# A hybrid decoder block on one core: the first stage pinned to a listed order on each engine, u products in halves, and the last tiles scaled on two engines

## The chip, the cores and the metric

The kernel runs on one core of one Trainium2 chip. The metric is the device time of one execution in microseconds (us). It is given as the median of several runs. The engines have short names: PE (TensorE, matrix products and transpositions), PEld (its weight loads), DVE (VectorE), ACT (ScalarE), POOL (GpSimd) and SP (SyncE, which issues most of the DMAs).

## The reference

The block takes `x` of 1024 tokens by 1024 channels and `mem` of 256 tokens by 1024 channels, all float32. Cut to its main lines:

```
u = rms_norm(x, norm_mix)
u_ssm, q, k, v, f_logit, gates = split(u @ w_in)          # widths 512, 512, 512, 512, 8, 2048
y = gelu(s5_ssm(u_ssm, ...))                              # diagonal state-space scan over the tokens
a, b = split(y @ w_glu);  out_a = a * sigmoid(b)
out_b = forgetting_attention(q, k, v, f_logit + b_forget) @ w_fox_o
ga, gb = split(sigmoid(gates))
h = x + (ga * out_a + gb * out_b) @ w_mix_out
h = h + cross_attention(rms_norm(h), rms_norm(mem, norm_mem_kv), w_mem_q, w_mem_kv, w_mem_o)
fa, fb = split(rms_norm(h) @ w_ffn_in)
h = h + (silu(fa) * fb) @ w_ffn_out
out = rms_norm(h) * norm_final
```

The part that matters first is how the stage at the head of the kernel makes `u` (transposed), the product `u_ssm`, and the keys and values of the memory tokens from `w_mem_kv`. The part that matters last is the final `rms_norm`.

## The kernel before, in words

**Splitting.** Products keep nearly float32 precision by splitting each operand into a high part (a cast to the reduced type float32r) and a low part (the difference). `split` (L176) makes both: ACT casts the high part (L177), and DVE, or POOL where that is asked for, subtracts it from the source (L178). A product of one 128-deep slice is then three matmuls (`mm3`, L165 to L169): high by high, high by low, low by high.

**Order.** The kernel is written in a framework that draws the instructions up at compile time. It gives every engine one queue of instructions in a fixed order, and adds the waits. Its scheduler goes by the order of the program as a priority, but lets a later instruction go ahead where an earlier one is, by its own estimate of durations, not ready yet. A helper can keep instructions behind a given one on the same engine (`behind`, L145).

**The first stage** (`stage_in`, L334 to L466) is a list of short steps, `ORDER_IN` (L41 to L47), carried out in that order by a table of functions (L456 to L466). A letter names the step and the rest its operands; `m` and `n` are the two memory tiles of 128 tokens and 0 to 7 the tiles of `x`:

- `F` fetches a tile; `G` fetches a gain row, and `B` spreads it over the 128 partitions with two small products on PE (L365) and two copies on ACT (L367).
- `Q` squares a tile on ACT and sums along the row (L373). `R` makes the reciprocal root (`rsqrt`, L186 to L203): an addition on DVE, the power on POOL (L196), and one Newton step of three small DVE instructions. One root serves one memory tile, or two tiles of `x`. `S` scales the tile by root and gain, on DVE (L216), or with `g` on ACT and POOL (L213, L214).
- `T` transposes half a tile (4 blocks of 128 by 128) into a PSUM bank on PE (L222); `E` evacuates that bank by splits into `uT` (or `mT`), a quarter tile of 128 by 256 each for `x`. The first half of a tile of `x` goes through the only bank called `misc`, the second through the two called `pv`.
- `D` fetches a block of weights: 0 to 3 are columns of `w_mem_kv` for the four heads' keys, 4 to 7 rows of it for the values, 8 to b the four blocks of 128 columns of `w_in` that make `u_ssm`. `W` splits it (with `g`, the low part on POOL). There are two buffers called `raw`, one called `xraw`, and four pairs for the split weights, so `W` waits until the product that used the pair four blocks earlier is done. The u weights (8 to b) were split through a permuted view, columns regrouped from (g n) to (n g).
- `K`, `V` and `U` are products. `K` is one head's keys (24 matmuls of 256 columns), `V` a quarter of the values (12 matmuls of 512 columns), `U` one block q of 128 channels of `u_ssm` for one half h of the tokens (24 matmuls of 512 columns). `k`, `v` and `u` bring the results out of PSUM.
- `Z` stores two of the four key and value tiles to DRAM. They share four slots (tag `kv`) with the gain rows before them and with the `us` tiles behind them, so the first `u` copies wait for the stores of `Z`.
- `u` (L446 to L452) copies a product to `us` on ACT, and after its second half stores block q to the DRAM tile `u_d` with one DMA of 512 KB.
- `X12` issues 12 small products whose result is not used, ahead of the first transpositions. `L0` fetches the parameters of the state-space branch (14 DMAs), `L1` transposes them on PE, and `P` carries out one piece of the preparation of that branch (`prepare`, from L1289, mostly small DVE instructions).

**The next stage** (`stage_ssm`, from L469) goes through 32 gate products of 24 matmuls each. Between them stand the steps of the state-space branch for each of the four blocks q: its weights on POOL and DVE (`weights`), the transposition of those (`turn_weights`, L1456, the first of them before the fifth gate product), the states (`states`, which reads `u_d` into `xg`, L1480), and the output.

**The last loop** (from L1160) is the second product of the feed-forward block, by seven sub-products (`ORDER` in L1102) over 11 pairs p, accumulated in eight PSUM banks. `o_add` (L1131 to L1136) adds a bank into the residual tile `Hf`, `square` (L1138) sums its squares on ACT, and `finish` (L1142 to L1149) makes the root, scales both halves of the tile on DVE by root and final gain (L1147), and stores each half with a DMA on SP (L1149). The last sub-product (n = 3) is finished tile by tile: for each of the tiles 0 to 3 its last nine matmuls, the sum, the squares, and `finish`.

Of the kernel before, what the change touches and what calls it, by code (L numbers as in the profile page):

```python
# [9 lines left out]
F32 = mybir.dt.float32  # L10
# [9 lines left out]
P = 128  # L20
# [46 lines left out]
def f32(ap):  # L67
    return ap.bitcast(F32)
# [47 lines left out]
        return self.pool.tile([P, 512], dt, tag="half", bufs=5, name=name)  # L116


class Block:
    BANKS = {"mm": 3, "sc": 2, "pv": 2, "misc": 1}  # L120

# [53 lines left out]

    def split(self, hi, lo, src, pool_lo=False):  # L176
        self.copied = self.A.copy(hi, src)  # L177
        (self.G if pool_lo else self.V).tensor_sub(lo, src, f32(hi))  # L178

    def rstd(self, src):  # L180
        ss = self.small.tile([P, 2], F32, name="ss")
# [36 lines left out]
    def turn(self, xs, b, bank):  # L218

        ps = self.bank(bank)  # L220
        for k in range(4):
            self.T.transpose(ps[:, k * P:(k + 1) * P], xs[:, (4 * b + k) * P:(4 * b + k + 1) * P], self.ident)  # L222
        return ps

    def turned(self, ps, b, act, t):
# [9 lines left out]
    def warm(self, n):  # L235

        ps = self.bank("misc")
        one = self.ident.bitcast(BF16)
        for _ in range(n):
            self.T.matmul(ps[:, :2 * P], one[:, :P], one, start=True, stop=True)  # L240


    def exp_parts(self, tile_, X):
# [90 lines left out]
def stage_in(B, xp, s5, x, mem, g_mix, g_kv, w_in, w_mem_kv, uT, u_d, kv_d):  # L334
# [8 lines left out]
    row, tiles, gain, ss, rs, raw, w, ps, us, kv = {}, {}, {}, {}, {}, {}, {}, {}, [], []  # L343
    names = {"m": -2, "n": -1, **{str(t): t for t in range(NT)}}

    def xtile(name="xt"):
# [13 lines left out]
    def gain_rows(i):  # L360
        gain[i] = xtile("gain")
        for c in range(2):
            cs = slice(512 * c, 512 * c + 512)
            p_ = B.bank("sc")
            T.matmul(p_, ones, row[i][:, cs], start=True, stop=True)  # L365
            with B.behind(B.copied if i else None):
                A.copy(gain[i][:, cs], p_)  # L367

    def square(t):
        if t % 2 == 0:  # L370
            ss[t // 2] = small.tile([P, 2], F32, name="ss2")
        with B.behind(B.copied if t in (0, 1) else None):
            A.activation(junk, tiles[t], AF.Square, scale=1.0 / 32, accum_out=ss[t // 2][:, t % 2:t % 2 + 1])  # L373

    def root(i):
        rs[i] = B.rsqrt(ss[-1][:, i % 2:i % 2 + 1] if i < 0 else ss[i])
# [48 lines left out]
    def kv_store(i0):  # L425
        for i in range(i0, i0 + 2):
            S.dma_start(kv_d[i], f32(kv[i]))
# [11 lines left out]
            cs = slice(t * 512, (t + 1) * 512)  # L439
            B.split(kv[2][:, cs], kv[3][:, cs], ps.pop(("v", t)))  # L440

    def ssm_in(q, h):
        ps["u", q, h] = B.bank("mm")
        B.gemm_t(ps["u", q, h], *w[8 + q], uT, h, 8)

    def ssm_out(q, h):  # L446
        if h == 0:
            us.append(xp.tile([P, D], F32, tag="kv", bufs=4, name="us"))
        uv = us[q].rearrange("p (t c) -> p t c", t=8)
        A.copy(uv[:, :, 64 * h:64 * h + 64], ps.pop(("u", q, h)).rearrange("p (c t) -> p t c", t=8))  # L450
        if h == 1:
            S.dma_start(u_d[q].rearrange("t p c -> p t c"), uv)  # L452

    prep = s5.prepare()

# [6 lines left out]
            "v": lambda a: values_out(), "Z": lambda a: kv_store(int(a)), "U": lambda a: ssm_in(int(a[0]), int(a[1])),  # L462
            "u": lambda a: ssm_out(int(a[0]), int(a[1])), "L": lambda a: s5.load(int(a)),
            "P": lambda a: next(prep, None), "X": lambda a: B.warm(int(a))}
# [75 lines left out]
def stage_tail(B, big, s2, sh, x, glu, aT, gate_d, kv_d, sums_d, w_fox_o, w_mix_out, g_mq, w_mem_q, w_mem_o, g_ffn,  # L540
# [563 lines left out]
    ops, Hf = {}, {}  # L1104
    ssq = small.tile([P, 2 * NT], F32, name="ssq", bufs=1)

    def o_get(m, behind=None):
# [23 lines left out]
    def o_add(n, i):  # L1131

        t, c, op = {1: (0, 0, ALU.add), 2: (0, 0, ALU.add), 6: (4, 0, ALU.add), 7: (4, 1, ALU.subtract),
                    5: (4, 1, ALU.subtract), 4: (4, 0, ALU.add), 3: (0, 1, ALU.subtract)}[n]
        h = Hf[t + i][:, 512 * c:512 * c + 512]
        V.tensor_tensor(out=h, in0=h, in1=sets[n in (2, 7, 4)][i], op=op)  # L1136

    def square(t, c):  # L1138
        A.activation(B.junk, Hf[t][:, 512 * c:512 * c + 512], AF.Square, scale=1.0 / 32,
                     accum_out=ssq[:, 2 * t + c:2 * t + c + 1])  # L1140

    def finish(t):  # L1142

        r = B.rsqrt(ssq[:, 2 * t:2 * t + 2], parts=2)
        for c in range(2):
            cs = slice(512 * c, 512 * c + 512)
            V.scalar_tensor_tensor(out=Hf[t][:, cs], in0=Hf[t][:, cs], scalar=r, in1=gfin[:, cs], op0=ALU.mult,  # L1147
                                   op1=ALU.mult)
            S.dma_start(out[t * P:(t + 1) * P, cs], Hf[t][:, cs])  # L1149
# [10 lines left out]
    for m, (n, p) in enumerate(seq):  # L1160
        if n == 3 and p >= NP - LAST:
            break
        for i in range(4):
            o_mm(m, i)
        if m + AHEAD < len(seq):
            o_get(m + AHEAD)
        if n < 3 and p in (2, 4, 6, 8):
            t = 4 * (n - 1) + p // 2 - 1
            Hf[t] = slot(name="hf")
            S.dma_start(Hf[t], h_d[t])  # L1170
        if p == NP - 1:
            for i in range(4):
                o_add(n, i)
                if n in (2, 5):
                    square(i if n == 2 else 4 + i, n // 3)
                if n == 4:
                    square(4 + i, 0)
                    finish(4 + i)
    for i in range(4):
        for m in range(len(seq) - LAST, len(seq)):  # L1180
            o_mm(m, i)
        o_add(3, i)
        square(i, 1)
        finish(i)


class Glu:
# [753 lines left out]
```

## Time and profile before

| | |
|---|---|
| time, median of 3 runs | 1569.69 us (1565.22 to 1571.21) |
| the profiled execution | 1565.22 us, span 1563.5 us |
| PE busy | 1524.3 us, 97% of the span |
| DVE, ACT, POOL busy | 1056.3, 679.0, 242.9 us |
| mean granted clock of PE | 0.992 |
| PE busy in the first 100 us | 87.3 us |
| first gate product on PE | at 104.14 us |
| last matmul ends | at 1553.24 us |

The profile is one execution. A view by groups gives, for each line and shape, the count, the busy time, the mean duration of one instruction, and the idle time of its engine just before, with what ended most of it. The view of waits says which line of an engine stood waiting and for which line of another. The timeline lists instructions by their start, with their length. The view by stretches gives each engine's busy time in a window, and PE's granted clock, the share of time in which the DMA engines were busy, and what they moved.

### The profile page before, as it was taken

How to read it: one execution, taken by the hardware profiler on the slowest of the kernel's cores; microseconds unless marked ns; L12 is line 12 of the kernel's file. 1: busy time of each engine (PE TensorE's matmuls, PEld its weight loads, DVE VectorE, ACT ScalarE, POOL GpSimd, SP SyncE). 2: the span in 40 equal slices, each digit the busy share in tenths (PEclk: the TensorE clock that was granted, in tenths of full speed). 3: DMA queues.
4: the chain of work that ended last, by engine and by line, in shares of the span. 5: the costliest groups of instructions: out<-in, count | busy, mean ns of one | idle time of the engine just before them, and what ended most of it. 6: DMA issues, size and time to landing. Idle time of an engine off the chain costs nothing.

```text
span 1563.5 us, 20462 instructions
## 1 busy us (share of the span) xinstructions
PE 1524.3 (97%) x7261; PEld 1250.4 (80%) x7261; DVE 1056.3 (68%) x1893; ACT 679.0 (43%) x1203; POOL 242.9 (16%) x323
## 2 busy tenths in 40 slices
PE   8899999999999899999999999999999999999997
PEld 6688888898777668888788778888888888888886
DVE  5947655544788786789756787777777766565555
ACT  6523333422566553444445654333333333354342
POOL 3135343200212122220102100000000000100001
PEclk9999999999999999999999999999999999999999
DMA  8655557642123637778431366444444554896642
GB/s 253 145 134 103 172 157 164 186 140 31 21 50 48 177 94 223 258 230 323 146 107 55 135 244 221 155 155 161 162 162 157 160 162 154 293 381 221 195 148 108
DMA packets 202586, 257.66 MB, mean 165 GB/s; under 512 B 35994, under 2 KB 127034, under 8 KB 201972
## 3 DMA queue, kind: packets, MB, share of 16 engines
q1 hardware_dynamic: 195860, 240.62, 51.4%
q10 hardware_dynamic: 6624, 15.73, 2.7%
q8 instruction: 57, 0.93, 0.2%
q14 instruction: 45, 0.37, 0.1%
HBM read 175.04 MB, written 83.20 MB: 165 GB/s over the span
## 4 chain that ended last, share of the span: by engine, by line
PE 82%; DVE 7%; DMA 4%; ACT 3%; issue 2%; POOL 2%; SPq 0%; DVEq 0%; POOLq 0%; ACTq 0%
PE mm L981 15%; PE pv L981 8%; PE mm L167 7%; PE mm L168 7%; PE mm L169 7%; PE mm L1128 5%; PE sc L1128 4%; PE sc L981 3%; PE pv L1128 3%; PE sc L169 2%; PE sc L168 2%; PE sc L167 2%; PE misc L1128 2%; PE mm L627 1%; PE pv L167 1%
## 5 line engine op out<-in xcount | busy, mean ns | idle before, releaser
L178 DVE TENSOR_TENSOR wlo<-raw,whi 128x1024 fp32r<-128x1024 f32 (+2 forms) x126 | 133.8, 1065 | 101.7 <-ACT whi L177 101.4
L177 ACT CAST whi<-raw 128x1024 fp32r<-128x1024 f32 (+2 forms) x127 | 115.9, 915 | 134.7 <-PE mm L168 36.0
L167 PE MATMUL mm<-uh,whi 128*128 128x512 f32 x344 | 137.5, 400 | 0.8 <-ACT whi L177 0.7
L178 DVE TENSOR_TENSOR ol<-or,oh 128x1024 fp32r<-128x1024 f32 x73 | 89.2, 1224 | 69.8 <-ACT oh L177 68.4
L169 PE MATMUL mm<-uh,wlo 128*128 128x512 f32 x344 | 135.4, 394 | 0.5 <-DVE wlo L178 0.5
L168 PE MATMUL mm<-ul,whi 128*128 128x512 f32 x344 | 135.5, 394 | 0.0
L177 ACT CAST oh<-or 128x1024 fp32r<-128x1024 f32 x73 | 76.8, 1053 | 100.3 <-PE mm L1128 33.3
L1013 POOL TENSOR_TENSOR g<-a,c 128x512 f32<-128x512 f32 x22 | 36.2, 1644 | 381.7 <-ACT a L1012 335.3
L196 POOL TENSOR_TENSOR r<-ms,mhalf 128x1 f32<-128x1 f32 (+1 forms) x30 | 21.7, 726 | 382.1 <-DVE ms L192 351.6
L1756 POOL TENSOR_TENSOR pl<-pf,ph 128x512 fp32r<-128x512 f32 (+1 forms) x32 | 39.5, 1236 | 243.4 <-DVE ph L1755 197.3
L169 PEld LDWEIGHTS mm<-uh,wlo 128*128 128x128 f32 x344 | 65.1, 189 | 14.8 <-DVE wlo L178 1.5
L167 PEld LDWEIGHTS mm<-uh,whi 128*128 128x128 f32 x344 | 65.3, 190 | 13.2 <-ACT whi L177 1.2
L168 PEld LDWEIGHTS mm<-ul,whi 128*128 128x128 f32 x344 | 65.1, 189 | 11.0
L1753 ACT ACTIVATE pf<-sc 128x512 f32<-128x512 f32 (+1 forms) x96 | 46.6, 490 | 46.9 <-DVE sc L1749 28.0
L981 PE MATMUL pv<-S3h,we 128*128 128x512 f32 x176 | 58.2, 390 | 0.1
L1759 DVE TENSOR_TENSOR pl<-pf,ph 128x512 fp32r<-128x512 f32 (+2 forms) x64 | 35.1, 549 | 10.0 <-ACT ph L1758 9.3
L1128 PE MATMUL mm<-oh 128*128 128x512 f32 x106 | 41.2, 389 | 0.0
L1128 PE MATMUL mm<-ol,oh 128*128 128x512 f32 x106 | 41.2, 389 | 0.0
L1128 PE MATMUL mm<-oh,ol 128*128 128x512 f32 x106 | 41.2, 389 | 0.0
L167 PE MATMUL mm<-yh,whi 128*128 128x512 f32 x104 | 41.1, 395 | 0.0
L168 PE MATMUL mm<-yl,whi 128*128 128x512 f32 x104 | 40.9, 393 | 0.0
L169 PE MATMUL mm<-yh,wlo 128*128 128x512 f32 x104 | 40.8, 393 | 0.0
(701 smaller groups left out, 4560.7 us busy)
## 6 DMA issues: line engine op xcount, KB each, us to landing
or<-c_d SPq DMA_DIRECT2D x77, 256.0 KB
wo<-in_w_ffn_out_dram SPq DMA_DIRECT2D x22, 512.0 KB
c_d<-g SPq DMA_DIRECT2D x44, 256.0 KB
t_d<-wo SPq DMA_DIRECT2D x44, 256.0 KB
or<-t_d SPq DMA_DIRECT2D x44, 256.0 KB
raw<-in_w_ffn_in_dram SPq DMA_DIRECT2D x20, 512.0 KB
rawb<-in_w_ffn_in_dram SPq DMA_DIRECT2D x20, 512.0 KB
raw<-in_w_in_dram SPq DMA_DIRECT2D x18, 512.0 KB
```

The costliest lines, as they stand in the source:

```text
L167: T.matmul(ps, lh, rh, start=first, stop=False)
L168: T.matmul(ps, lh, rl, start=False, stop=False)
L169: T.matmul(ps, ll, rh, start=False, stop=last)
L177: self.copied = self.A.copy(hi, src)
L178: (self.G if pool_lo else self.V).tensor_sub(lo, src, f32(hi))
L196: self.G.tensor_tensor(out=r, in0=v, in1=self.mhalf[:, 0:n], op=ALU.pow)
L981: T.matmul(ps, l_[:, k, :], r_, start=first and k == 0 and i == 0, stop=k == 3 and i == 2, skip_group_check=True)
L1013: G.tensor_mul(g[:, 512:], a1, c1)
L1128: T.matmul(ps, l_[:, gi], r_[:, 512:], start=n < 3 and p == 0 and k == 0 or n == 7 and p == 0 and k == 0, stop=p == NP - 1 and k == 2, ski ...
L1753: self.exp = A.activation(pf[:, off:], ps[:, off:], AF.Exp)
L1756: G.tensor_sub(pl[:, off:], pf[:, off:], f32(ph[:, off:]))
L1759: V.tensor_sub(pl[:, off:], pf[:, off:], f32(ph[:, off:]))
```

## The change

The first stage gets a new order, in which the steps stand otherwise and the warm-up step `X` and all steps with `g` are gone. While the list is carried out, every instruction on DVE, ACT, PE and SP is kept in program order on its engine (`InOrder`), so the scheduler no longer lets a later one go ahead; POOL stays free. From `L1` on the engines are free again, but the instructions of `L1` and `P` are kept behind the last low half on DVE and behind the last transposition on PE. The helpers that kept single ACT instructions behind a cast go.

The product `U` is cut in halves over its depth: `Uqhs` with s = 0 needs only the first half (four slices) of each tile's channels. The u weights are split as they lie, and the regrouping from (n g) to (g n) moves into the store, which becomes eight DMAs of 16 partitions for each block. The order of the four blocks is free.

In the last loop, a tile below 4 has the first half of its channels multiplied by the final gain on POOL ahead of time (after n = 2, when its squares are summed). `finish` then scales that half by the root on ACT and stores it from ACT's queue, and DVE scales only the second half. `finish` of a tile comes after the sum and squares of the next one, and is kept behind them.

The diff, cut to its core:

```diff
 ORDER_IN = """
-G0 G1 Fm Fn B0 X12 Qm D1 Qn Rm D0 Sm F1 Tm0 Tm1 Rn Em0 Em1 Sn F0 D2 Tn0 Tn1 W0 En0 En1 B1 Q0 F2 F3 D3 Q1 W1g K0 F4 F5 K1 R0
-S0 T00 T01 k0 E00 Q2 W2g D4 F6 F7 D8 E01 S1 T10 Q3 W3 k1 D5 K3 K2 W4 E10 W5 D6 R1 k2 T11 k3 S2 Q4 V0 S3g T30
-E11 D7 Q5 T20 R2 T21 E21 E20 S4 E30 W6 D9 W7 T40 V1 S5 E40 T31 V2 E31 W8 T41 V3 Da Db Z0 L0 T50 Q6 v T51 W9
-E51 U00 Z2 Q7 E41 R3 S6 u00 L1 Wa T60 E50 S7 T61 T70 Wbg E61 U10 E60 T71 E70 E71 P0 U20 u10 u20 P1 U21 U11 U30
-P2 u30 U31 u11 u31 U01 u21 P3 P4 P5 u01
+Fn G0 G1 Fm Qn Qm Rn Rm B0 D4 F0 Sn Sm F1 W4 B1 Tn0 Q0 En0 Tm1 Tn1 D2 Q1 R0 Tm0 D1 Em0 D6 F7 S0 V0 W1 F2 D0 Em1
+En1 W2 W6 T00 E00 K1 T01 Q2 Q7 F3 S1 K2 W0 Q3 T10 D5 F4 D3 K0 R1 T11 D8 W5 E10 V1 k2 k1 S3 W3 V2 E11 D7 E01 S2
+T30 D9 k0 Db W7 T31 K3 T21 E30 E31 Da Q4 T20 F5 W8 E20 W9 Wa V3 U000 U200 k3 Q5 E21 F6 U001 R2 S4 Wb S5 U201 L0
+Q6 Z0 T41 T40 R3 U100 S6 u00 E40 u20 T50 E50 v U101 S7 T60 T61 E41 U300 E60 T71 E61 T70 T51 E71 Z2 U301 E70 E51
+U010 u10 u30 U210 U011 U310 U311 U211 u01 U110 u31 U111 u21 u11 L1 P0 P1 P2 P3 P4 P5
 """
...
+class InOrder:
+
+    def __init__(self, tc, engine):
+        self.tc, self.engine = tc, engine
+
+    def __getattr__(self, name):
+        op = getattr(self.engine, name)
+        return lambda *a, **k: self.tc.keep_in_program_order(op(*a, **k))
...
+    free = {e: getattr(B, e) for e in "VATS"}
+    pinned = {e: InOrder(B.tc, free[e]) for e in "VATS"}
+    vars(B).update(pinned)
...
     def wsplit(i, pool):
         hl = [B.wpool.tile([P, WSLOT], F32R, tag=t_, name=t_)[:, :D] for t_ in ("whi", "wlo")]
-        if i < 8:
-            B.split(*hl, raw.pop(i), pool)
-        else:
-
-            B.split(*[t_.rearrange("p (k n g) -> p k n g", k=8, n=16) for t_ in hl],
-                    raw.pop(i).rearrange("p (k g n) -> p k n g", k=8, g=8), pool)
+        B.split(*hl, raw.pop(i), pool)
...
-    def ssm_in(q, h):
-        ps["u", q, h] = B.bank("mm")
-        B.gemm_t(ps["u", q, h], *w[8 + q], uT, h, 8)
+    def ssm_in(q, h, s):
+        if s == 0:
+            ps["u", q, h] = B.bank("mm")
+        for k in range(4 * s, 4 * s + 4):
+            B.mm3(ps["u", q, h], w[8 + q][0][:, k, :], w[8 + q][1][:, k, :], *uT.rhs(k, h), k == 0, k == 7)
...
-        if h == 1:
-            S.dma_start(u_d[q].rearrange("t p c -> p t c"), uv)
+        if last:
+            for g in range(8):
+                S.dma_start(u_d[q].rearrange("t (n g) c -> g n t c", g=8)[g], uv[16 * g:16 * g + 16])
...
     for step in ORDER_IN.split():
-        acts[step[0]](step[1:])
+        if step == "L1":
+            vars(B).update(free)
+        with B.behind(B.lowered if B.V is free["V"] else None), B.behind(B.flipped if B.V is free["V"] else None):
+            acts[step[0]](step[1:])
...
     def finish(t):
 
-        r = B.rsqrt(ssq[:, 2 * t:2 * t + 2], parts=2)
-        for c in range(2):
+        with B.behind(added[-1]):
+            r = B.rsqrt(ssq[:, 2 * t:2 * t + 2], parts=2)
+        if t < 4:
+            with B.behind(squared[-1]):
+                A.activation(Hf[t][:, :512], Hf[t][:, :512], AF.Copy, scale=r)
+            A.dma_start(out[t * P:(t + 1) * P, :512], Hf[t][:, :512])
+        for c in range(t < 4, 2):
...
+                if n == 2:
+                    G.tensor_mul(Hf[i][:, :512], Hf[i][:, :512], gfin[:, :512])
...
         o_add(3, i)
         square(i, 1)
-        finish(i)
+        if i:
+            finish(i - 1)
+    finish(3)
```

More of the change, by code (lines that the diff above doesn't have):

```diff
@@ L177, in split @@
         self.copied = self.A.copy(hi, src)
-        (self.G if pool_lo else self.V).tensor_sub(lo, src, f32(hi))
+        self.lowered = (self.G if pool_lo else self.V).tensor_sub(lo, src, f32(hi))
     def rstd(self, src):
@@ L221, in turn @@
         for k in range(4):
-            self.T.transpose(ps[:, k * P:(k + 1) * P], xs[:, (4 * b + k) * P:(4 * b + k + 1) * P], self.ident)
+            self.flipped = self.T.transpose(ps[:, k * P:(k + 1) * P], xs[:, (4 * b + k) * P:(4 * b + k + 1) * P], self.ident)
         return ps
@@ L233, in norm_turn @@
             self.turned(self.turn(xs, b, banks[b]), b, act, t)
[L235 to L240, printed above, removed]
     def exp_parts(self, tile_, X):
@@ L342, in stage_in @@
     mT = Act(xp, "mT", 4, 8, ML, kg=4, name="m")
-    row, tiles, gain, ss, rs, raw, w, ps, us, kv = {}, {}, {}, {}, {}, {}, {}, {}, [], []
+    row, tiles, gain, ss, rs, raw, w, ps, us, kv = {}, {}, {}, {}, {}, {}, {}, {}, {}, []
     names = {"m": -2, "n": -1, **{str(t): t for t in range(NT)}}
@@ L365, in gain_rows @@
             T.matmul(p_, ones, row[i][:, cs], start=True, stop=True)
-            with B.behind(B.copied if i else None):
-                A.copy(gain[i][:, cs], p_)
+            A.copy(gain[i][:, cs], p_)
     def square(t):
[L370 to L373, printed above, removed]
+        if t // 2 not in ss:
+            ss[t // 2] = small.tile([P, 2], F32, bufs=5, name="ss2")
+        A.activation(junk, tiles[t], AF.Square, scale=1.0 / 32, accum_out=ss[t // 2][:, t % 2:t % 2 + 1])
     def root(i):
@@ L1103, in stage_tail @@
     seq = [(n, p) for n in ORDER for p in range(NP)]
-    ops, Hf = {}, {}
+    ops, Hf, squared, added = {}, {}, [], []
     ssq = small.tile([P, 2 * NT], F32, name="ssq", bufs=1)
```

15 lines of the change are left out of this document (8 added, 7 removed).

## The prediction

> **What bounds the kernel now.** I read the page first, then the waits of PE in the first 90 us, then busy times by stretch.
>
> ```profile
> span 1563.5 us, 20462 instructions
> ...
> PE 1524.3 (97%) x7261; PEld 1250.4 (80%) x7261; DVE 1056.3 (68%) x1893; ACT 679.0 (43%) x1203; POOL 242.9 (16%) x323
> ```
>
> The profiled execution took 1565.22 us, 1.7 more than its span; the median of the three runs is 1569.69, so I work in microseconds saved and take them off the median. Half a per cent, about what a measurement of this kernel can tell from no change, is 7.8 us. PE is busy for 97% of the span: 39.2 us are left, and the change touches the two places where most of them lie, the first 100 us and the last 10.
>
> ```profile
> PE sc L167 <- ACT whi L177: 1.7, 1, 1.7
> PE misc L222 <- DVE ul L178: 1.3, 1, 1.3
> PE pv L222 <- DVE ul L178: 1.3, 1, 1.3
> PE misc L222 <- DVE xt L216: 1.2, 1, 1.2
> ```
>
> These are single waits, each for another product: a schedule that is now and then late, not an engine that is too slow. The stretches say the same (columns: length, busy us of PE, of its weight loads, DVE, ACT, POOL, then PE's granted clock, DMA share, GB/s):
>
> ```profile
> 22.00:24.00 2.00, 1.35 (x12) 1.15 (x10) 1.19 (x4) 2.00 (x5) 1.33 (x2) 1.00 1.01 399
> 24.00:26.00 2.00, 0.78 (x5) 0.58 (x6) 1.93 (x4) 0.77 (x2) 0.00 (x0) 1.00 0.96 343
> 26.00:28.00 2.00, 2.00 (x15) 2.00 (x14) 2.00 (x3) 1.42 (x3) 0.00 (x0) 0.65 1.01 392
> 28.00:30.00 2.00, 2.00 (x11) 2.00 (x11) 1.53 (x7) 1.68 (x4) 0.70 (x1) 0.50 1.09 312
> 30.00:32.00 2.00, 2.00 (x19) 2.00 (x19) 1.92 (x3) 0.70 (x2) 0.00 (x0) 1.00 1.00 140
> ...
> 16.75:104.14 87.39, 79.33 (x406) 66.10 (x406) 66.37 (x200) 43.66 (x79) 18.63 (x15) 0.96 0.69 169
> ```
>
> The last row runs from the first memory product to the first gate product:
>
> ```profile
> 13.92 0.60 PE L222 MATMUL pv<-ident,xt 128*128 128x128 f32 x4
> 16.75 0.51 PE L167 MATMUL mm<-mh,whi 128*128 128x256 f32 x2 [2.23 <-ACT mh L177]
> ...
> 103.91 0.39 PE L169 MATMUL mm<-uh,wlo 128*128 128x512 f32 x1
> 104.14 0.39 PE L167 MATMUL sc<-uh,whi 128*128 128x512 f32 x1
> ```
>
> Of its 87.39 us PE idles 8.06 (87.39 - 79.33) and loses 4% of the clock, 3.5 us. What it has to do at full clock is 75.8 us. So the first stage can give back at most 11.6 us after 16.75.
>
> **The change: the start of the stage.** Durations are those of the old trace.
>
> ```profile
> 2.33 7.16 PE L365 MATMUL sc<-row,ones 1*128 1x512 f32 x8 [2.33 <-DMA row<-in_norm_mem_kv_dram]
> ...
> 6.59 1.06 ACT L373 ACTIVATE junk<-xt 128x1024 bf16<-128x1024 f32 x1
> ...
> 7.78 0.15 DVE L194 TENSOR_SCALAR ms<-ss 128x1 f32<-128x1 f32 x1 [6.64 <-ACT junk L373]
> ...
> 9.20 1.28 DVE L216 SCALAR_TENSOR_TENSOR xt<-xt,r,gain 128x1024 f32<-128x1024 f32 x1
> ```
>
> The first tile is now fetched ahead of the gain rows, so Qn comes at about 5 us, not at 6.59 or later, and Qm ends at 7.3. Two roots of 1.4 each (7.78 to 9.20) and two scalings bring Sm's end to 11.3 on DVE. On PE the second row product (B1, half of the 7.2 us) now stands ahead of the first transposition, and it needs a bank that the first gain copy (7.3 to 7.8) frees: 7.8 to 11.3. On ACT the last gain copy ends at 11.9, and Q0, En0, Q1 and Em0 follow (1.06 a square, 0.5 an evacuation), to 15.0; on DVE R0 (1.6, with its trip to POOL), to 16.1, then Em0's low half, to 16.7. V0 thus starts at about 16.75, where the first key product starts today: nothing gained, 1 us either way.
>
> **Capacity after that.** The groups by shape of the first 104 us (count, busy us, mean ns, idle before):
>
> ```profile
> L216 DVE SCALAR_TENSOR_TENSOR xt<-xt,r,gain 128x1024 f32<-128x1024 f32 x9 | 11.4, 1280 | 0.2
> L373 ACT ACTIVATE junk<-xt 128x1024 bf16<-128x1024 f32 x10 | 10.8, 1082 | 0.1
> ...
> L178 DVE TENSOR_TENSOR wlo<-raw,whi 128x1024 fp32r<-128x1024 f32 x8 | 9.8, 1221 | 9.7 <-ACT whi L177 9.7
> ...
> L177 ACT CAST whi<-raw 128x1024 fp32r<-128x1024 f32 x9 | 9.5, 1060 | 13.2 <-PE mm L168 13.2
> ...
> L177 ACT CAST whi<-wr 128x1024 fp32r<-128x1024 f32 x4 | 8.1, 2030 | 1.1 <-PE sc L169 0.9 <-ACT uh L177 0.2
> ...
> L178 DVE TENSOR_TENSOR ul<-misc,uh 128x256 fp32r<-128x256 f32 x16 | 6.7, 419 | 1.3 <-ACT uh L177 1.1
> ...
> L178 DVE TENSOR_TENSOR wlo<-wr,whi 128x1024 fp32r<-128x1024 f32 x3 | 5.9, 1975 | 0.0
> ```
>
> Unpermuted u weights cost as the others: ACT saves 4 x (2.03 - 1.06) = 3.9 us, DVE 3 x (1.98 - 1.22) = 2.3. POOL's three low halves and one gain product of today go to DVE, 3 x 1.22 + 1.28 = 4.9. From 16.75 on DVE then holds 8 scalings (10.2), 11 weight halves (13.4), 32 quarter tiles at 0.42 (13.4), about 3 for the memory keys, values and tiles, and 3 roots at 1.6 (4.7): about 46 us, to 63. The last eight half products (U010 to U111) are the only ones behind its last evacuation; they are 8 x 12 matmuls at 0.23 (103.91 to 104.14) = 22 us, so PE comes to them after 75.8 - 22 - 1 (the preparation's transposes) = 52.8 us, at 69.5 or later. DVE has 6 us to spare; ACT, with less to do, more. Capacity therefore lets PE run on; what counts is order.
>
> **Waits that the pinned order makes.** An engine that stands holds everything listed behind it. I checked each step's margin. K1 needs the low halves of Em1 and En1 (20.3; PE is there at 19.9 at full clock). K0, V1, K3 and V3 have 1 to 5 us. Tightest is the third u block: the four u loads move at the slow rate of the 30 to 32 row, 140 GB/s, 3.5 us each, so Da lands near 43, just as ACT comes to it; F5 and F6 follow. Then the store: L0's fourteen small DMAs now stand ahead of Z0 on SP.
>
> ```profile
> 43.15 4.47 SPq L427 DMA_DIRECT2D kv_d<-kv  x2
> 47.68 0.86 SPq L1258 DMA_DIRECT2D prow<-in_lam_re_dram  x1
> ...
> 58.69 0.96 SPq L1274 DMA_DIRECT2D dbc<-in_d_skip_dram  x1
> ...
> 105.67 0.37 SPq L452 DMA_DIRECT2D u_d<-us  x1
> ...
> 109.55 0.34 SPq L1480 DMA_DIRECT2D xg<-u_d  x1
> ```
>
> L0 holds SP for 12.0 us (47.68 to 58.69 + 0.96), and the copy u00 on ACT needs the slot that Z0 frees. With F6 issued by 40 to 43 (today the last u load is out when the first kv store follows at 43.15), Z0 goes at 52 to 55 and lands some 3.6 later (109.55 is what waited for the store issued at 105.67): 56 to 59, while ACT stands at u00 from 53. Behind it stand E40's copies, and T50 needs their bank. PE is at T50 at 59: it waits 0 to 4.3 us. I take **2.0 us for all new waits**, nearer to the small end, since the margins elsewhere are there; 0 and 4.3 stay as bounds.
>
> **The clock.** The 12 warm-up matmuls go. In the new walk PE stands from 13.2 to 16.75, and the rows show half clock from 26.6 to 30 (0.65 is 1.4 of 2 us at half) after a stretch (22 to 26) in which PE was busy 2.13 of 4 us. One such half-rate stretch of 3.4 us costs 1.7; I take **one, 1.7** (bounds 0 and 3.4, the 3.5 us of today). The Trainium skill (TensorE: Matmul & The Clock Gate, HAM oscillation) holds that the clock falls only after an idle gap of over about 3.4 us. By that rule the dropped warm-up costs the same one stretch, and later waits cost no clock; the trace differs, since its longest gap ahead of the fall is 1.20 us, so by the rows a cluster of waits could add a second 1.7, and 1560.0 would be 1561.7.
>
> Sum of the stage: 75.8 + 1.7 + 2.0 = 79.5 instead of 87.39, **7.9 us saved**; bounds 11.6, and 87.39 - (75.8 + 3.4 + 4.3) = 3.9.
>
> **The u stores** become 32 issues instead of 4, 28 x 0.37 = 10.4 us of SP, between the gate weights' loads. The first reader comes over 20 us after the first store; it waits for the last one, as today. I cost this nothing; without that cover it would be 3 us.
>
> **The tail.**
>
> ```profile
> 1547.15 0.69 DVE L1136 TENSOR_TENSOR hf<-hf,sc 128x512 f32<-128x512 f32 x1 [10.39 <-PE sc L1128]
> ...
> 1549.57 0.16 DVE L200 TENSOR_TENSOR rt<-r 128x1 f32<-128x1 f32 x1 [0.66 <-POOL r L196]
> ...
> 1552.85 0.39 PE L1128 MATMUL mm<-oh,ol 128*128 128x512 f32 x1
> ...
> 1554.87 0.68 DVE L1136 TENSOR_TENSOR hf<-hf,mm 128x512 f32<-128x512 f32 x1
> ...
> 1558.99 1.42 DVE L1147 SCALAR_TENSOR_TENSOR hf<-hf,r,gbc 128x512 f32<-128x512 f32 x2
> ```
>
> PE ends at 1553.24, yet the last sum is added at 1554.87, behind tile 1's two scalings, and the last scaling ends at 1560.41. DVE's first tile shows the shortest way: add at 1547.15, root back at 1549.57, scaling 0.6 later, 3.0 in all. From 1553.3 that gives 1556.3, and 0.7 for a half on each engine: 1557.0, 3.4 saved at best. Each tile still costs DVE an add, a root and one half, so I walk to 1558.5: **1.9 saved** (1.0 to 3.4). The four POOL products with the gain run in the loop ahead, where DVE's 10.39 us of idle time hides them.
>
> Total: 7.9 + 1.9 = 9.8. The profiled execution would be 1555.4; from the median, 1569.69 - 9.8, **1560 us**.
>
> **Rivals.** (B) In-order waits take half of it: everything late as bounded, 3.9 + 1.0 = 4.9 saved, 1565. For it: Z0 behind L0; against it: DVE's 6 us.
>
> (C) No wait, full clock, best tail: 11.6 + 3.4 = 15.0, 1555.
>
> (D) Slower. The state-space preparation L1 now follows all u products.
>
> ```profile
> 61.83 0.26 PE L1279 MATMUL misc<-ident,prow 48*128 48x48 f32 x1
> ...
> 125.90 0.60 PE L1456 MATMUL pv<-ident,fre 128*128 128x128 f32 x4
> ```
>
> ```profile
> 110.12 1.15 POOL L1407 TENSOR_TENSOR fim<-w,w 128x448 f32<-128x448 f32 x1
> ```
>
> From its first transpose (61.83) to fim (111.27) are 49.4 us, and PE reads fim at 125.90. If the transposes go only after the last u product, at about 95, and the chain shrinks only by the 6.4 us of splits that DVE did within it, fim ends at 138, while PE, 7.9 us early, wants it at 118: 20 us of waiting if nothing else stands there, 10 us slower than before: 1580. It decides from a chain longer than 33 us. Against it: POOL idled 12 us in that chain, and 28 gate products are there to fill in.
>
> (E) The list does not bind, since the scheduler's own order was about this one: no change, 1570.
>
> **Chances.** Forecast 0.55, its own range 1556 to 1563; B 0.20; C 0.12; D 0.08; E 0.05. Faster by over 0.5% (below 1561.8): four fifths of the forecast's 0.55, and C: 0.56. Slower by over 0.5%: D and a little of B's tail, 0.09. The same: the rest, 0.35. The range, 1554 to 1568, takes in the forecast, C, and B, and leaves out D, E and run scatter.
>
> **What would show it.** Right: the first gate product at about 96.2 instead of 104.14, PE's waits between 16.75 and there about 2 us in total, one stretch at half clock from V0; u-weight casts of 1.06 us on ACT; ACT's longest wait at u00, for a store; the last scaling 1.9 us nearer to PE's end. Wrong: V0 later than 18; a wait of PE at the state-space transposes of fre or fim; ACT waiting for u-weight loads for more than 4 us.

## The result and the profile after

The changed kernel takes 1578.11 us (median of 5 runs, 1576.11 to 1580.12) beside 1569.69 us (5 runs, 1565.22 to 1571.21) for the kernel before. The ratio is 1.0058, 95% interval 1.0040 to 1.0076: slower by some 9 us, where the prediction had 10 us faster. The profiled executions lie further apart than the medians, since the one of the changed kernel took 1580.12 us and the one of before 1565.22 us; with their spans they differ by 14.9 us, and the account below is of those. By the medians the difference is 8.4 us; the other 6.5 are scatter between executions, so the sizes below are those of one pair and not averages.

The page of the changed kernel, first line and busy times:

```profile
span 1578.4 us, 20474 instructions
...
PE 1527.3 (97%) x7249; PEld 1252.1 (79%) x7249; DVE 1063.1 (67%) x1893; ACT 677.3 (43%) x1206; POOL 245.3 (16%) x323
```

PE's share is the same 97%; the page does not show where 15 us went. The stretches do (length, busy us of PE, PEld, DVE, ACT, POOL, then PE's clock, DMA share, GB/s). First the changed kernel, from its first memory product to its first gate product, and from there to the evacuation of the last gate product:

```profile
17.18:96.55 79.37, 75.50 (x402) 62.93 (x402) 44.88 (x79) 36.35 (x73) 2.17 (x4) 1.00 0.65 159
96.55:325.34 228.79, 216.69 (x1069) 183.59 (x1069) 150.02 (x305) 79.15 (x124) 91.72 (x193) 0.96 0.62 151
```

The second stretch in the kernel before:

```profile
104.14:312.18 208.04, 207.68 (x1065) 176.94 (x1064) 123.51 (x180) 78.04 (x123) 83.98 (x186) 1.00 0.63 158
```

So the first stage did what was forecast (79.37 us instead of 87.39), and PE came to the gate products 7.6 us earlier. The stage of the gates, in which the change edits nothing, then took 228.79 us instead of 208.04: 20.75 us were lost in this pair of executions, where the prediction had looked only in a rival. From there to PE's end the two differ by another 2.0 us, which I did not trace.

What happened at the border of the two stages, on PE in the changed kernel (start, length, line, operation, idle time before it and what ended that):

```profile
96.36 0.26 PE L1294 MATMUL misc<-ident,prow 48*128 48x48 f32 x1
96.55 0.50 PE L177 MATMUL sc<-uh,whi 128*128 128x512 f32 x1
...
118.72 0.39 PE L179 MATMUL mm<-uh,wlo 128*128 128x512 f32 x1
122.55 1.11 PE L1471 MATMUL pv<-ident,fre 128*128 128x128 f32 x4 [3.44 <-POOL ES L1445]
123.45 0.47 PE L1477 MATMUL misc<-cb_re,fre 128*128 128x32 f32 x2
123.74 0.77 PE L177 MATMUL mm<-uh,whi 128*128 128x512 f32 x1
124.31 0.63 PE L178 MATMUL mm<-ul,whi 128*128 128x512 f32 x1
127.54 1.11 PE L1471 MATMUL pv<-ident,fim 128*128 128x128 f32 x4 [2.60 <-POOL fim L1422]
...
131.29 0.77 PE L179 MATMUL mm<-uh,wlo 128*128 128x512 f32 x1
```

The first transposition of the state-space preparation goes at 96.36, at the side of the first gate product; before it went at 61.83. After four gate products PE stands 3.44 us for `fre`, does two matmuls of the fifth product, and stands 2.60 us for `fim`. (The row names `ES` as what ended the first wait; that is a small filling of 0.10 us right behind `fre` on POOL, and `fre` itself ends at 122.49.) POOL and DVE show the chain between:

```profile
117.66 1.14 POOL L1420 TENSOR_TENSOR w<-ld_re,bb_re 128x448 f32<-128x448 f32 x1 [59.06 <-DVE bb_re L1375]
...
121.37 1.12 POOL L1422 TENSOR_TENSOR fre<-w,w 128x448 f32<-128x448 f32 x1
...
126.36 1.13 POOL L1422 TENSOR_TENSOR fim<-w,w 128x448 f32<-128x448 f32 x1
```

```profile
DVE par L1296 <- PE misc L1294: 6.3, 1, 6.3
```

```profile
119.00 1.21 DVE L188 TENSOR_TENSOR wlo<-raw,whi 128x1024 fp32r<-128x1024 f32 x1
127.52 0.69 DVE L1431 TENSOR_TENSOR w<-la_re,cT_re 128x512 f32<-128x512 f32 x1 [7.31 <-POOL fim L1422]
...
128.73 1.21 DVE L188 TENSOR_TENSOR wlo<-raw,whi 128x1024 fp32r<-128x1024 f32 x1
```

DVE, through with the first stage, waited 6.3 us for that transposition. POOL had stood idle for 59 us and began only with DVE's result `bb_re`, 21.3 us behind the transposition. The two rows of `wlo` are the low halves of the weights of the fifth to eighth gate products: DVE makes them behind 22 us of preparation, and the second only behind its own wait of 7.3 us for `fim`.

All waits of PE between 94 and 215 us, after; in the kernel before this view holds one wait, of 0.4 us:

```profile
PE pv L1502 <- ACT F L1472: 4.1, 1, 4.1
PE pv L1471 <- POOL ES L1445: 3.4, 1, 3.4
PE pv L1471 <- POOL fim L1422: 2.6, 1, 2.6
PE pv L1545 <- ACT Tt L1489: 2.0, 1, 2.0
```

And the clock (the third number from the right) around them:

```profile
122.55:127.54 4.99, 2.39 (x8) 1.67 (x9) 0.02 (x1) 1.08 (x2) 4.99 (x11) 0.50 0.45 114
127.54:140.00 12.46, 12.46 (x54) 11.00 (x55) 6.01 (x10) 3.56 (x6) 9.09 (x30) 0.67 0.26 65
164.17:170.00 5.83, 5.83 (x42) 5.45 (x43) 1.89 (x3) 4.36 (x7) 4.90 (x18) 1.00 0.23 85
...
190.00:195.00 5.00, 3.87 (x17) 3.87 (x18) 4.92 (x8) 3.22 (x5) 0.00 (x0) 0.53 0.94 358
195.00:200.00 5.00, 5.00 (x19) 4.01 (x19) 4.45 (x6) 2.58 (x7) 1.27 (x1) 0.79 0.37 117
```

The waits sum to 12.1 us. The granted clock is the share of full speed that PE was given, so the missing share of its busy time is the cost: 1.2 + 4.1 behind the first pair of waits, 1.8 + 1.1 behind the wait of 4.1. That is 8.2, and 20.3 in all, of the 20.75 lost.

The tail of the changed kernel:

```profile
1567.98 0.39 PE L1134 MATMUL mm<-oh,ol 128*128 128x512 f32 x1
```

```profile
1569.12 0.75 DVE L1158 SCALAR_TENSOR_TENSOR hf<-hf,r,gbc 128x512 f32<-128x512 f32 x1
...
1571.84 0.75 DVE L1158 SCALAR_TENSOR_TENSOR hf<-hf,r,gbc 128x512 f32<-128x512 f32 x1
...
1573.97 0.75 DVE L1158 SCALAR_TENSOR_TENSOR hf<-hf,r,gbc 128x512 f32<-128x512 f32 x1
```

```profile
1574.03 0.72 ACT L1154 ACTIVATE hf<-hf,r 128x512 f32<-128x512 f32 x1 [1.40 <-DVE r L212]
```

The last scaling ends at 1574.75, 6.4 us behind PE's end (1568.37); before it was 7.2 (1560.41 - 1553.24). That is 0.8 gained. But the span ends 3.65 us behind the last scaling instead of 3.09, so that 0.2 is left. The last store now leaves from ACT; whether that makes the difference was not tested.

### The profile page after: what moved, and what is told of

It reads as the page before. It is cut to its first block, busy times and chain, and to the rows that moved or that the text cites. A ratio compares the mean times of both kernels' runs of the same rounds, so it can differ in the third digit from the quotient of the medians.

```text
span 1578.4 us, 20474 instructions
## 1 busy us (share of the span) xinstructions
PE 1527.3 (97%) x7249; PEld 1252.1 (79%) x7249; DVE 1063.1 (67%) x1893; ACT 677.3 (43%) x1206; POOL 245.3 (16%) x323
## 4 chain that ended last, share of the span: by engine, by line
PE 78%; DVE 8%; DMA 4%; ACT 4%; POOL 3%; issue 3%; SPq 0%; POOLq 0%; ACTq 0%; DVEq 0%
PE mm L987 14%; PE pv L987 7%; PE mm L177 6%; PE mm L178 6%; PE mm L179 6%; PE mm L1134 5%; PE sc L1134 4%; PE sc L987 3%; PE pv L1134 3%; PE mm L126 2%; PE sc L177 2%; PE sc L178 2%; PE sc L179 2%; PE misc L1134 2%; PE mm L633 2%
## 5 line engine op out<-in xcount | busy, mean ns | idle before, releaser
L188 DVE TENSOR_TENSOR wlo<-raw,whi 128x1024 fp32r<-128x1024 f32 (+2 forms) x121 | 127.2, 1054 | 99.3 <-ACT whi L187 98.9
L177 PE MATMUL mm<-uh,whi 128*128 128x512 f32 x280 | 113.4, 405 | 0.5 <-ACT whi L187 0.4
L179 PE MATMUL mm<-uh,wlo 128*128 128x512 f32 x280 | 111.5, 399 | 0.5 <-DVE wlo L188 0.5
L178 PE MATMUL mm<-ul,whi 128*128 128x512 f32 x280 | 111.6, 399 | 0.0
L179 PEld LDWEIGHTS mm<-uh,wlo 128*128 128x128 f32 x280 | 53.7, 192 | 12.6 <-DVE wlo L188 1.5
L177 PEld LDWEIGHTS mm<-uh,whi 128*128 128x128 f32 x280 | 54.0, 193 | 10.8 <-ACT whi L187 0.9
L178 PEld LDWEIGHTS mm<-ul,whi 128*128 128x128 f32 x280 | 53.9, 193 | 8.9
L1241 POOL TENSOR_TENSOR sg<-sg,ga 128x512 f32<-128x512 f32 x16 | 32.0, 2016 | 71.4 <-DVE sg L1234 40.9
L177 PE MATMUL sc<-uh,whi 128*128 128x512 f32 x104 | 41.5, 399 | 0.0
L179 PE MATMUL sc<-uh,wlo 128*128 128x512 f32 x104 | 41.0, 395 | 0.0
```

The costliest lines, as they stand in the source:

```text
L177: T.matmul(ps, lh, rh, start=first, stop=False)
L178: T.matmul(ps, lh, rl, start=False, stop=False)
L179: T.matmul(ps, ll, rh, start=False, stop=last)
L188: self.lowered = (self.G if pool_lo else self.V).tensor_sub(lo, src, f32(hi))
L1241: self.B.G.tensor_mul(self.out[j][:, cs], self.out[j][:, cs], ga)
```

## The experiments

Three theories were put against each other. **Theory 1**: the preparation, now behind the last u product, ends too late for a place in the gate stage that did not move; the whole loss follows from it. **Theory 2**: only the waits at `fre` and `fim` follow from it, the later ones come from the second block's load of `xg`, which stands behind weight loads. **Theory 3**: the pinned order or the 32 stores cost the time. Each kernel was run in five rounds beside the kernel before; the medians of before were 1567.2 to 1568.6 us, so the ratios are what is to be compared. The last two columns are in us from the start of the span, each from one profiled execution: where the first gate product starts, and where the evacuation of the last one starts.

| kernel | median us | ratio to before (95%) | first gate product | last gate evacuation |
|---|---|---|---|---|
| before (profile) | 1569.69 | 1 | 104.14 | 312.18 |
| changed | 1578.11 | 1.0058 (1.0040 to 1.0076) | 96.55 | 325.34 |
| changed, preparation early | 1566.26 | 0.9995 (0.9982 to 1.0008) | 97.75 | 313.04 |
| changed, transposes placed later | 1580.01 | 1.0076 (1.0057 to 1.0096) | 96.23 | 324.93 |
| before, preparation last | 1582.55 | 1.0093 (1.0073 to 1.0112) | 104.87 | 330.67 |
| before, new tail | 1566.48 | 1.0002 (0.9990 to 1.0014) | | |
| preparation in two parts | 1568.38 | 1.0005 (0.9993 to 1.0017) | 101.86 | 313.46 |
| preparation early, xg earlier | 1563.68 | 0.9981 (0.9963 to 0.9999) | 97.78 | 308.03 |
| changed, not pinned | 1585.37 | 1.0112 (1.0091 to 1.0134) | 100.13 | 327.59 |
| before, 32 stores | 1566.23 | 0.9990 (0.9975 to 1.0004) | 103.80 | 311.83 |
| preparation earliest, xg earlier | 1560.97 | 0.9958 (0.9943 to 0.9973) | 98.76 | 306.43 |
| changed, xg earlier | 1574.10 | 1.0051 (1.0031 to 1.0071) | 96.85 | 320.76 |
| before, xg earlier | 1566.46 | 0.9990 (0.9976 to 1.0003) | 104.85 | 312.26 |

**The preparation early.** One move in the list, with the preparation pinned like the rest:

```
-U010 u10 u30 U210 U011 U310 U311 U211 u01 U110 u31 U111 u21 u11 L1 P0 P1 P2 P3 P4 P5
+U010 L1 P0 P1 P2 P3 P4 P5 u10 u30 U210 U011 U310 U311 U211 u01 U110 u31 U111 u21 u11
```

> The changed kernel with one move: the state-space preparation (its transposes and its four steps on VectorE) stands right behind the first of the last eight half products of u, in the pinned part, instead of behind the last one; everything else as changed. Theory 1 (the late preparation costs what the stage saved, because the transposes of fre and fim stand at a fixed place, behind the fourth gate product): the preparation's first transpose goes at about 77 instead of 96.4, fim ends before 112, PE's waits of 3.4 and 2.6 us at the transposes and the half clock behind them go, and with them what follows from them (2.0 at the output products, 4.1 at the second block's states); the first gate product stays at about 96.5; 16 to 20 us under the changed kernel, near 1559. Theory 2 (only the first block's waits come from it, the later 2.0 and 4.1 us come from the queue of stores and loads): 12 us less, near 1566. Theory 3 (the pinned order or the 32 stores cost it, not the place of the preparation): within 3 us of the changed kernel, 1575 to 1581.

Measured: 0.63% less than the changed kernel by the ratios, about 10 us. The first transposition went at 76.90, `fim` ended at 115.6 (expected before 112), and the waits at both transposes are gone. What is left between 94 and 215 us:

```profile
PE pv L1500 <- ACT F L1470: 3.9, 1, 3.9
PE pv L1543 <- ACT Tt L1487: 0.9, 1, 0.9
```

The late preparation is thus a cause, and the larger one; the pinned order and the 32 stores are still there, so theory 3 falls as the cause. But 1566 is theory 2's number, not theory 1's 1559: the lead of 6.4 us at the first gate product was gone at the last one (313.04 against 312.18). The wait of 3.9 us lies at the second block's states. ACT and SP around it:

```profile
167.58 0.58 ACT L1470 COPY F<-pv 128x512 f32<-128x512 f32 x1
178.07 0.35 ACTq L493 DMA_DIRECT2D gate_d<-gs  x1
178.46 0.59 ACT L1470 COPY F<-pv 128x512 f32<-128x512 f32 x1 [10.30 <-DMA xg<-u_d]
```

```profile
166.00 2.71 SPq L163 DMA_DIRECT2D raw<-in_w_in_dram  x2
168.82 0.45 SPq L1493 DMA_DIRECT2D xg<-u_d  x1
```

ACT's queue stands at a gate store until the load of `xg` has landed, and behind it stands the copy of `F`. The two have nothing to do with each other, but in the trace both signal their landing on one semaphore (105), and ACT waits on it directly ahead of the store. The load itself was issued behind two loads of weights, which SP could issue only when DVE had freed their slots. The tile of the first block that `xg` overwrites had been free from about 156.

**The transposes placed later.** In the changed kernel, `turn_weights` and `states` of the first block stand two gate products later in the program, and with `states` the `weights` of the second block.

```
-        todo[4 + 7 * q] = [lambda q=q: s5.turn_weights(q)]
+        todo[4 + 7 * q + 2 * (q == 0)] = [lambda q=q: s5.turn_weights(q)]
```

> The changed kernel with the first block's transposes of fre and fim, and its states, two gate products later (behind the sixth and seventh instead of the fourth and fifth); the preparation stays behind the last u product. Theory 1: the two products, 10.9 us, cover the chain of the preparation (fim ended 8.8 us after the place where PE first wanted fre), so the waits of 3.4 and 2.6 us and the half clock behind them go: 8 to 13 us under the changed kernel, 1565 to 1570; part of it comes back if the first block's work then collides with the second's, which keeps its place. Theory 3 (the pinned order or the stores): within 3 us of the changed kernel.

A miss: 1580, not 1565 to 1570, and not to be told from the changed kernel by the intervals. The number alone would fit theory 3; the trace shows why theory 1's repair did not take. The transposes of `fre` stayed where they were (122.23): the scheduler lets a later instruction go ahead only where the earlier ones are not ready by its estimate, so the fifth product was taken to be unready as well. Only those of `fim` moved, to 137.36. The wait for `fim` went, and a longer one came when the first block's outputs ran into the delay:

```profile
PE pv L1545 <- ACT Tt L1489: 7.7, 1, 7.7
PE pv L1471 <- POOL ES L1445: 3.4, 1, 3.4
```

Placing the reader later did not help. What it shows against the prediction: no gate product was drawn ahead into the gap in front of `fre`, even where the program had two of them ahead of it.

**The kernel before with its preparation last.** `L1` and `P0` to `P5` go to the end of the old list; nothing else.

> The kernel before with one move: the preparation behind the last u product, nothing pinned, the old stores and the old tail. Theory 1: its first transpose goes at about 104 instead of 61.8, the chain of some 31 us ends fim at about 135, while PE wants it at 126: waits at the transposes and half clock behind them, 8 to 20 us over the kernel before, 1578 to 1590. Theory 3 (what the changed kernel lost is the pinned order's doing): within 4 us of the kernel before.

1582.55, within theory 1's bracket (by the ratio 0.93%, some 15 us, over the kernel before). The transposition went at 104.69, `fim` ended near 142, and PE shows the wait by itself, without pinning, halves or stores:

```profile
PE pv L1456 <- POOL fre L1407: 9.7, 1, 9.7
PE pv L1456 <- POOL fim L1407: 1.1, 1, 1.1
```

**The tail alone.** The kernel before with the new `finish`, `square` and POOL products.

> The kernel before with the new tail alone. My prediction had 1.9 us (1.0 to 3.4); the two traces show the last scaling ending 6.4 us after PE instead of 7.2, so 0.8: 1569, not to be told from no change by the time, and the distance from PE's end to the last scaling 6.4 us again.

No change in time (1.0002), and 6.4 us from PE's end to the last scaling (1563.70 - 1557.34), with 3.8 us from there to the end of the span. The tail brings nothing that can be measured.

**The preparation in two parts.** `L1` goes up behind the last tile's scaling (`S7 L1 T60`), the steps `P` stay where the early preparation has them.

> The run with the preparation moved up (e1_prep_early), and its transposes and copies moved up once more, behind the scaling of the last tile; the four steps on VectorE then start as soon as VectorE is through with the last tile. There the chain of the preparation still ended fim at 115.6, and the tables behind it (EC, ES) at 141.2, later than the states of the first block wanted them (PE had these at 127.7 to 130), so that the lead of 6.4 us was gone by the scans. Theory 1 (the rest of the lead is lost to the same chain, on VectorE and GpSimd): 3 to 5 us earlier tables give 2 to 5 us more, 1561 to 1564. Theory 2 (the rest is lost at the second block's load of xg, behind two weight loads): no change, 1565 to 1568.

It did not gain. Pinned there, the transposes stopped PE and DVE in turn, and the first gate product came at 101.86, 4.1 us later than with the early preparation. `fim`, though, was made at the same time (114.80 against 114.47), and the last gate product was evacuated at 313.46 against 313.04. So 4 us in the first stage made no difference at the end of the second: its end did not go with PE's arrival. Between the two theories this run does not decide, since the chain of the preparation, which it was to bring forward, ended no earlier.

**The load of xg ahead of the weights.** On the early preparation; `fetch` issues the load two gate products earlier, and the weight loads are kept behind it.

```
+        todo[3 + 7 * q] = [lambda q=q: s5.fetch(q, u_d)]
...
+            with B.behind(getattr(s5, "fetched", None)):
+                gate_weights(j // 2 + 1)
```

> The run with the preparation moved up (e1_prep_early), and each block's load of xg issued ahead of the gate weights' loads that stood in front of it on SP. Theory 2: PE's wait of 3.9 us at the second block's states and the half clock behind it go (they cost 3.9 and about 3.4 us there): 4 to 7 us more, 1559 to 1562. Theory 1: xg lands earlier, but the states then wait for something else of VectorE's or GpSimd's: under 2 us, 1564 to 1568.

The wait of 3.9 us went, no half clock was left in the first 340 us, and the last gate product was evacuated at 308.03 instead of 313.04: 5.0 us in the trace, at the low end of theory 2's 4 to 7. In the time it was 0.14% by the ratios, about 2 us, with overlapping intervals, so the bracket of 1559 to 1562 was missed (1563.68).

**Not pinned.** The changed kernel with `InOrder` passing every operation through; the same list, halves, weights, stores and tail.

> The changed kernel without the pinning: the same new list, halves, weights, stores and tail, but the scheduler orders each engine's work by its own costs; the preparation stays behind the last u product. If the pinned order gives the first stage its 7.6 us, the first gate product comes back to 100 to 104 and the time goes to 1581 to 1586; if the new list and the halves give it, the first gate product stays near 96.5 and the time within 3 us of the changed kernel's 1578.

1585.37, and the first gate product at 100.13:

```profile
100.13 0.50 PE L177 MATMUL sc<-uh,whi 128*128 128x512 f32 x1
```

In these executions, of the 7.6 us that the first stage gained, 3.6 go with the pinning and 4.0 stay with the list, the halves and the weights. The pinned order costs nothing: without it the kernel is slower by 0.54%.

**32 stores in the kernel before.**

> The kernel before with each of its four u stores cut in eight, by 16 partitions: 28 more issues on SP and nothing else. My prediction costs them nothing, since the first reader comes over 20 us later, and 3 us without that cover. The changed kernel's SP was held by its 32 stores for 17 us. Theory 3 (the stores take part in the loss): 3 us or more over the kernel before; theories 1 and 2: within 2 us of it.

No cost (0.9990). From the first to the last of them SP needs 26.2 us here, and 17.0 in the changed kernel. That is not all issuing: one store takes 0.43 us (median), all of them 14.3 here and 13.4 in the changed kernel, and for the rest SP waits for the copies of `us`. The stores here are not regrouped as in the changed kernel, so it is their number that was tested:

```profile
83.57 26.23 SPq L453 DMA_DIRECT2D u_d<-us  x32
109.90 0.95 SPq L153 DMA_DIRECT2D raw<-in_w_in_dram  x2
111.69 0.34 SPq L1481 DMA_DIRECT2D xg<-u_d  x1
```

**Both repairs, the preparation earliest.** As with the earlier `xg`, and `L1` ahead of `U010` instead of behind it.

> Both repairs together, the preparation one half product earlier still: its transposes right behind the last tile's evacuation on VectorE, ahead of the first of the last eight half products, and each block's load of xg ahead of the gate weights' loads (e6_xg_earlier had the second repair and the preparation behind that half product; it gave 1563.7, its first gate product at 97.8 and its last gate product's evacuation at 308.0 instead of 312.2). Theory 1: the preparation starts 2.5 us earlier, the waits of 0.7 to 0.8 us that are left at the output products shrink: 0 to 2 us less, 1561 to 1564. Against it: PE stands about 1 to 2 us at the transposes, as it did when they came earlier still.

1560.97: faster than before by 0.42% (0.27% to 0.57%), the best of all. PE does not stand once between its first gate product and the evacuation of the last:

```profile
98.76:306.43 207.67, 207.67 (x1065) 176.91 (x1064) 136.16 (x220) 79.25 (x124) 94.51 (x193) 1.00 0.68 166
```

The lead of 5.4 us at the first gate product is 5.75 at the last. The stage that lost 20.75 us now runs without a wait and at full clock. The interval overlaps that of the early preparation with the earlier `xg` (0.9963 to 0.9999), so the time does not show what the last half product adds.

**The load of xg alone, in the changed kernel and in the kernel before.**

> The changed kernel with each block's load of xg ahead of the gate weights' loads, and nothing else; the preparation stays behind the last u product. Theory 2 (the wait of 4.1 us at the second block's states, and the half clock behind it, 2.9 us, come from the load of xg behind two weight loads, not from the preparation): 5 to 7 us under the changed kernel, 1571 to 1573. Theory 1 (they come from the late preparation, too): within 2 us of it.

> The kernel before with each block's load of xg ahead of the gate weights' loads, and nothing else: whether what that move gave is to be had without the change. PE waited 0.4 us for the second block there, so within 1 us of the kernel before; if it is 3 us or more faster, the move and not the change made the gain of e6_xg_earlier.

In the changed kernel the wait of 4.1 us at the second block's states went, with the preparation as late as in the changed kernel. The other three stayed (3.4, 2.6, 2.1), new ones of 0.7, 0.6 and 0.2 came later, and the last gate product was evacuated 4.6 us earlier. The ratios (1.0051 and 1.0058) cannot tell that from no change, so the time bears out neither theory, and the trace bears out theory 2, a little under its 5 to 7. In the kernel before the move is worth nothing that can be measured (0.9990, an interval that reaches over 1), so it alone is not what made the kernel with both repairs faster. The traces show the margin. In the kernel before, the second load of `xg` is issued 9.8 us ahead of PE's arrival at the second block's states (170.55 and 180.37), and PE waits 0.4. In the changed kernel it is 6.3 us (180.75 and 187.05), with the early preparation 6.4 (168.82 and 175.18). In the changed kernel PE comes there later than before, and the load later still.

## Why the prediction was wrong

The term that was wrong was not one of the sum; it was a cost that the sum did not have. Point by point:

- **Start of the stage: right in its number, in part by luck.** V0 at 17.18, said 16.75 with 1 us either way. But the second row product ended at 13.1, not at 11.3, and PE did not stand behind it: it transposed until 16.5.
- **The stage: right in its total, by luck: two errors cancel.** It took 79.37, said 79.5. The work was 75.50 (said 75.8). The new waits were 3.9 us (79.37 - 75.50), 1.9 more than the 2.0 that were said, within the bounds; the half-clock stretch of 1.7 did not come. They were many and small, with none at `u00` or T50, where I had put them; ACT's longest wait in the stage, 7.3 us, was for PE and harmless:

```profile
PE mm L126 <- DVE wlo L126: 1.3, 2, 0.8
PE misc L126 <- DVE ul L126: 0.7, 1, 0.7
```

  The clock is 1.00 throughout, and the gap ahead of V0 from which I had the half-clock stretch is the one that PE filled with transpositions. The rule that I had weighed from the Trainium skill (TensorE: Matmul & The Clock Gate, HAM oscillation: no idle gap of PE over about 3.4 us) agrees with this stage, whose longest gap was 0.8 us. It does not agree with every run: the last section has a fall behind a gap of 2.32 us.

- **Sums of the stage.** DVE's five terms add to 44.7 us, not to 46 (it was busy 44.88 in the stage), and 512 KB at 140 GB/s take 3.7 us, not 3.5. Neither changes the forecast.

- **u weights: right.** The casts took 1.05 us each, as the row by shape shows:

```profile
L126 ACT CAST whi<-wr 128x1024 fp32r<-128x1024 f32 x4 | 4.1, 1049 | 0.0
```

- **u stores at no cost: right** as far as their number goes, by the run with 32 stores in the kernel before.
- **The tail: mis-sized.** 1.9 was said, 0.8 measured at the last scaling and 0.2 at the end of the span. I walked from the shortest tile. On the chip a tile costs 2.72 us (1569.12 to 1571.84, above) where it cost 2.79 (1556.20 to 1558.99): half a scaling left DVE, but the next tile's sum took its place ahead of the root, and the root's trip to POOL still stands in between.
- **What follows the stage: wrong.** The forecast carried the stage's 7.9 us to the end of the kernel. The step that failed is the overlap in rival D, "28 gate products are there to fill in", by which the forecast put the moved preparation at nothing. They did not fill in. Each engine's order is fixed before the kernel runs; `fre` stands behind the fourth gate product, in both kernels some 22 us behind the first (104.14 to 125.90 before), and the fifth product's own weights are split on DVE behind the preparation. The preparation started with the first gate product, its chain took 31.1 us (96.36 to 127.49), and no chain over 22 us fits there. In its place PE waited 6.0 us at the two transposes and lost 5.3 to half clock behind them, over half of the 20.75 us that the stage lost. The other half of that sentence was right: the chain did compress, from 49.4 us.
- **The price of D** was 20 us of waiting less 10; it gave 1580, and 1578 was measured. That is near by luck: the chain was to take 43 us and took 31.1. (Its row at 125.90 is the transposition of `fre`, too; `fim` is read at 126.34.) The parts were different: 6.0 us of waiting at the two transposes, 5.3 of half clock behind them, and 2.0 + 4.1 + 2.9 at the outputs and the second block. Its point of decision, a chain longer than 33 us, was too high, because it counted the wait and neither the clock nor what follows. One sentence of defence made 0.08 of a mechanism whose place and chain I had already worked out.
- **What was not seen at all**: that the second block's load of `xg` came just in time before (PE waited 0.4 us), so that a smaller margin between load and PE shows as a wait. With the preparation early and that load moved, 0.42% is gained, some 6.6 us of the 9.8 forecast. A move of the load to another queue was not tried.

## What to carry to other kernels

Work that is moved behind the end of a stage starts with the next one. Look up where its first reader stands in the next stage, in the order as drawn up, and compare that distance (here 22 us) with the chain (here 31 us). Filling work counts only if it is ahead of the reader on its engine and its own operands do not wait for the same chain.

A lead won in one stage is worth what the next stage's transfers and buffers allow. Here a lead of 7.6 us turned into a loss. It took two moves, of the preparation and of a load, until a lead (5.4 us then) passed through the next stage whole.

## What the runs showed of the hardware

- The clock: the longest gap in the changed first stage was 0.8 us, and 3.9 us of idle time in all left it at 1.00; so did a single gap of 2.0 us (ahead of 164.17). Gaps of 3.44 and 4.1 us were followed at once by 0.50 and 0.53. In the preparation in two parts, a gap of 2.32 us was followed by 0.52:

```profile
178.09:180.41 2.32, 0.00 (x1) 0.01 (x1) 0.20 (x1) 0.64 (x2) 2.00 (x2) 1.00 1.02 409
180.41:184.00 3.59, 3.59 (x17) 3.59 (x18) 3.51 (x5) 2.58 (x4) 0.00 (x0) 0.52 0.83 318
```

  Without the pinning, a gap of 2.36 us (ahead of 47.15) left the clock at 1.00, and in the kernel before it fell at 26 to 30 us behind gaps of 1.20 us and less. So the length of a single gap does not decide alone; what does stays open.
- Half clock cost nearly as much as the waits that led to it (8.2 us beside 3.44 + 2.60 + 4.08).
- One small store of 64 KB took SP 0.43 us to issue. In the kernel before, 32 of them cost no time that could be measured: ACT waited 6.7 us for one of them, but PE, from there to the end of the next stage, for none.
- A store on ACT's queue stood until a load on SP's queue had landed that signals on the same semaphore, 10.3 us in one run, and held the copy behind it that PE was waiting for.
